# One core's hybrid attention and HGRN2 layer: products of 512 columns over both token streams, and x and the context loaded first

## The chip, the cores and the metric

The kernel runs on one core of one Trainium2 chip. The metric is the device time of one execution in microseconds (us); the time before is the median of three runs.

## The reference

One layer over 256 latent tokens `x` with a prefix of 256 context tokens `ctx`, all in float32, model width 2048. Both token streams are normed, modulated and multiplied by the same input weights. Only the latent stream goes on to attention queries, gates, output projection and SwiGLU.

```python
mod = silu(c) @ w_mod + b_mod                 # 2048 x 12288
mod_c = silu(c_ctx) @ w_mod + b_mod
h  = modulate(rmsnorm(x, g0), sh_a, sc_a)
hc = modulate(rmsnorm(ctx, g0), csh_a, csc_a)
p, pc = h @ w_in, hc @ w_in                   # q, kv and rope latents, HGRN2 q, ff, fb, i, g, two gates
attn_l = block_attention(q_l, [k_c, k_l], [v_c, v_l])
hgo_c, s_f, s_b = hgrn2_bidirectional(ctx parts, 0, 0)
hgo_l = hgrn2_bidirectional(latent parts, s_f, s_b)
out = (sig(gate0) * (attn_l @ w_br_mla) + sig(gate1) * (norm(hgo_l) * silu(g) @ w_br_hgrn)) @ w_out
x = x + gt_a * rmsnorm(out, g1)
h = modulate(rmsnorm(x, g2), sh_f, sc_f)
x = x + gt_f * rmsnorm((silu(h @ w_a) * (h @ w_b)) @ w_ffn_out, g3)
```

## The kernel before

Everything is float32. An operand of a large product is split into a rounded part H (ScalarE's cast to fp32r) and a rest L (VectorE's subtraction), and a product is the sum of three: H with H, H with L, L with H. Tokens lie on the free axis: a stream's h for one of the 16 blocks k of 128 model rows is a tile of 128 partitions by 2 parts by 256 tokens. The latent stream's 16 tiles are `hA`, the context's 16 are `hB`.

**Start.** The first modulation (`w_mod`'s columns for shift and scale of the first norm) comes in 32 tiles of 1 MB (`raw<-in_wm_dram`), in the groups of `GROUPS`: a group of nk blocks has 2·nk tiles. TensorE multiplies each tile with c (`pm`, L256). At the end of a group ScalarE copies the sum (`row`, L266), TensorE turns it (`pt`, L269), and VectorE and ScalarE make h of the group's blocks for both streams (L195 to L197). Meanwhile six blocks of 128 output columns of `w_in` (`pre`, whose weights come in 16 pieces `rw<-in_wst_dram` on GpSimd's queue) are built up block k by block k in six PSUM banks (L125, called from `pre_mm`). The norms of x and ctx (`norm_x`) are squares on ScalarE, sums on VectorE, a product with ones (`ptok`, L143), and a product that spreads the root over the partitions (`pbc`, L155).

**Heads.** Then come the attention latents and the eight HGRN2 heads. Each head has five blocks of `w_in` of 128 columns (`project`); three of them are for both streams, two for the latent stream alone. Of the blocks for both streams, those of the latents of k and v, of the rope part and of head 0 are `pre`; heads 1 to 7 have 21 more. For each k a block for both streams has six products of 256 columns (`mm3`, L125), a block for one stream three. VectorE's chains of the forget gate run beside it.

**Gates, attention, merge, output, SwiGLU.** The 32 gate blocks (`gates`) use `mm_wide` (one product of 512 columns over H and L side by side, L129, and one of 256, L130). Their results wait in 16 tiles `sgt` until the merge (L713 to L719). Output projection and the second half of the SwiGLU (`project_tok`, L778) have products of 512 columns.

The order on each engine comes from a scheduler that simulates the program at build time; the queues run in that order. Raw weights (`raw`) have three buffers of 1 MB, filled by SyncE's queue.

## Time and profile before

| | |
|---|---|
| median of 3 runs | 1767.45 us (1766.27 to 1767.64) |
| the profiled execution | 1768.12 us, of which its span 1766.30 us |
| TensorE (PE) busy | 1725.0 us, 98% of the span |
| weight loads (PEld) busy | 1528.4 us, 87% |
| VectorE (DVE) busy | 1110.0 us, 63% |
| ScalarE (ACT) busy | 800.1 us, 45% |
| moved by DMA | 374.64 MB, mean 212 GB/s |

A busy PE says only that products lie one behind the other: each row's duration has its draining in it, which the next product overlaps. What a product costs is read from the distance of two starts. Between the end of the span's last instruction and the device time lie 1.82 us that no view shows.

### The profile page before, as it was taken

How to read it: one execution, taken by the hardware profiler on the slowest of the kernel's cores; microseconds unless marked ns; L12 is line 12 of the kernel's file. 1: busy time of each engine (PE TensorE's matmuls, PEld its weight loads, DVE VectorE, ACT ScalarE, POOL GpSimd, SP SyncE). 2: the span in 40 equal slices, each digit the busy share in tenths (PEclk: the TensorE clock that was granted, in tenths of full speed). 3: DMA queues.
4: the chain of work that ended last, by engine and by line, in shares of the span. 5: the costliest groups of instructions: out<-in, count | busy, mean ns of one | idle time of the engine just before them, and what ended most of it. 6: DMA issues, size and time to landing. Idle time of an engine off the chain costs nothing.

```text
span 1766.3 us, 26819 instructions
## 1 busy us (share of the span) xinstructions
PE 1725.0 (98%) x10976; PEld 1528.4 (87%) x10976; DVE 1110.0 (63%) x1703; ACT 800.1 (45%) x1178; POOL 38.6 (2%) x57
## 2 busy tenths in 40 slices
PE   4999999999999999999999899999999999999998
PEld 2779999999999888888998698888888888888886
DVE  4335777766678766666775687776445555555556
ACT  4224433333334655555444554444444444334443
POOL 2100000000000000000110000000000000000000
PEclk9999999999999999999999999999999999999999
DMA  9985456555556555566765457777555555555563
GB/s 361 331 320 194 140 178 208 191 191 170 175 173 231 212 182 207 177 248 232 260 228 200 169 178 275 281 276 257 195 192 185 188 191 190 192 191 189 181 215 130
DMA packets 56459, 374.64 MB, mean 212 GB/s; under 512 B 6512, under 2 KB 6800, under 8 KB 13072
## 3 DMA queue, kind: packets, MB, share of 16 engines
q1 hardware_dynamic: 53424, 365.06, 59.1%
q0 software_dynamic: 2048, 6.29, 1.1%
q8 instruction: 86, 1.41, 0.3%
q10 hardware_dynamic: 864, 1.57, 0.2%
q14 instruction: 37, 0.30, 0.0%
HBM read 370.79 MB, written 2.11 MB: 211 GB/s over the span
## 4 chain that ended last, share of the span: by engine, by line
PE 97%; DVE 1%; DMA 1%; ACT 1%; issue 0%; SPq 0%; DVEq 0%; ACTq 0%
PE ps L125 20%; PE pst L778 18%; PE psf L129 18%; PE psf L130 9%; PE ps L129 7%; PE psb L713 5%; PE pre L125 4%; PE ps L130 3%; PE pm L256 2%; PE psf L872 1%; PE psS L656 1%; PE po L679 1%; PE psS L653 1%; DMA xt<-in_xT_dram 1%; PE pv L628 1%; PE pq L612 1%
## 5 line engine op out<-in xcount | busy, mean ns | idle before, releaser
L102 DVE TENSOR_TENSOR wL<-raw,wH 128x1024 fp32r<-128x1024 f32 (+1 forms) x492 | 597.5, 1217 | 462.4 <-ACT wH L100 461.3
L100 ACT CAST wH<-raw 128x1024 fp32r<-128x1024 f32 (+1 forms) x492 | 508.7, 1037 | 748.7 <-PE ps L125 182.1
L129 PE MATMUL psf<-h,wH 128*128 128x512 f32 x1344 | 475.1, 399 | 0.0
L130 PE MATMUL psf<-h,wL 128*128 128x256 f32 x1344 | 377.5, 281 | 0.0
L129 PEld LDWEIGHTS psf<-h,wH 128*128 128x128 f32 x1344 | 252.6, 188 | 62.8
L125 PE MATMUL ps<-hA,wH 128*128 128x256 f32 x1312 | 254.6, 285 | 0.0
L130 PEld LDWEIGHTS psf<-h,wL 128*128 128x128 f32 x1344 | 253.9, 189 | 0.2
L125 PEld LDWEIGHTS ps<-hA,wH 128*128 128x128 f32 x1312 | 204.8, 192 | 1.2 <-issue 0.5
L125 PE MATMUL ps<-hA,wL 128*128 128x256 f32 x656 | 187.3, 286 | 0.0
L129 PE MATMUL ps<-hA,wH 128*128 128x512 f32 x512 | 183.8, 400 | 0.0
L778 PE MATMUL pst<-wH,gA 128*128 128x512 f32 x576 | 166.6, 389 | 0.0
L321 DVE CUSTOM_DVE_ANT_0 raw<-raw,cb 128x2048 f32<-128x2048 f32 x64 | 146.0, 2281 | 29.9 <-DMA raw<-in_wm_dram 29.7
L130 PE MATMUL ps<-hA,wL 128*128 128x256 f32 x512 | 144.0, 282 | 0.0
L125 PE MATMUL ps<-hB,wH 128*128 128x256 f32 x672 | 137.2, 284 | 0.0
L778 PEld LDWEIGHTS pst<-wH,gA 128*128 128x128 f32 x576 | 108.0, 188 | 22.3
L125 PEld LDWEIGHTS ps<-hA,wL 128*128 128x128 f32 x656 | 125.7, 192 | 0.5 <-issue 0.5
L129 PEld LDWEIGHTS ps<-hA,wH 128*128 128x128 f32 x512 | 96.0, 188 | 22.9 <-issue 1.3
L125 PEld LDWEIGHTS ps<-hB,wH 128*128 128x128 f32 x672 | 105.0, 192 | 0.0
L778 PE MATMUL pst<-wL,gA 128*128 128x512 f32 x288 | 101.4, 389 | 0.0
L130 PEld LDWEIGHTS ps<-hA,wL 128*128 128x128 f32 x512 | 96.5, 189 | 2.6 <-DVE mx L658 1.1
L125 PE MATMUL ps<-hB,wL 128*128 128x256 f32 x336 | 95.2, 283 | 0.0
L778 PE MATMUL pst<-wH,mg 128*128 128x512 f32 x256 | 74.4, 389 | 0.0
(432 smaller groups left out, 2189.3 us busy)
## 6 DMA issues: line engine op xcount, KB each, us to landing
raw<-in_wm_dram SPq DMA_DIRECT2D x96, 1024.0 KB, 5.0
raw<-in_wfi_dram SPq DMA_DIRECT2D x84, 1024.0 KB, 4.9
raw<-in_win_dram SPq DMA_DIRECT2D x73, 1024.0 KB, 4.9
raw<-in_wfo_dram SPq DMA_DIRECT2D x44, 1024.0 KB, 4.8
raw<-in_wbr_dram SPq DMA_DIRECT2D x16, 1024.0 KB, 5.0
raw<-in_wout_dram SPq DMA_DIRECT2D x16, 1024.0 KB, 4.9
rw<-in_wst_dram POOLq DMA_DIRECT2D x16, 256.0 KB, 5.8
raw<-in_wqk_dram SPq DMA_DIRECT2D x4, 1024.0 KB, 4.9
```

Of the source, the lines that this page charges most:

```text
L100: nc.scalar.copy(H, raw[:, o:o + n])
L102: nc.vector.tensor_tensor(L, raw[:, o:o + n], H.bitcast(F32), op=ALU.subtract)
L125: nc.tensor.matmul(o, l, r, start=(first and i == 0), stop=(last and i == len(seq) - 1))
L129: nc.tensor.matmul(ps, w[0], act.rearrange("p e t -> p (e t)"), start=first, stop=False)
L130: nc.tensor.matmul(ps[:, 0:T], w[1], act[:, 0, :], start=False, stop=last)
L256: nc.tensor.matmul(pm[32 * (k % 4):32 * (k % 4) + 32, 0:n], cst[:, k], raw[:, kk * n:(kk + 1) * n], start=(k < 4), stop=(k >= KD - 4))
L321: nc.vector.tensor_tensor_reduce(out=raw, in0=raw, in1=cbt[0], scale=1.0, scalar=0.0, op0=ALU.mult, op1=ALU.add, accum_out=mod2[:, i // KD ...
L612: nc.tensor.matmul(pq[:, i * T:(i + 1) * T], l, r, start=(k == 0 and i == 0 and z == 0), stop=(k == 3 and i == 1 and z == 2))
L628: nc.tensor.matmul(pv[:, i, :], ckvs[:, k, l, ts_], r, start=(i == 0 and k == 0 and z == 0), stop=(i == 1 and k == 1 and z == 2))
L653: nc.tensor.matmul(psS, qn[a][:, i * T + qb * P:i * T + (qb + 1) * P], kn[b], start=(n == 0), stop=False)
L713: nc.tensor.matmul(ps[:, br * T:(br + 1) * T], l, r, start=(br == 0 and k == 0 and z == 0), stop=(br == 1 and k == NH - 1 and z == 2))
L778: mm = nc.tensor.matmul(ps[hf], l, r, start=(k == 0 and n == 0), stop=(k == nk - 1 and n == 2))
```

## The change

Both streams' h go into one tile `hx` of 128 partitions by stream, block k, part and 256 tokens. A block for both streams now has, for each k, three products of 512 columns; their moving operand is two runs of 256 columns, one of each stream, which lie 32 KB apart on a partition. SyncE's queue loads x and the context before the first tiles of the modulation, and the weights of blocks k = 0 and 1 too; `GROUPS` begins with four groups of one block instead of two. The norm is spread by one product with ones whose result stands in every partition; root and reciprocal are then taken over 128 x 256. As the h tiles are gone, other tiles move: the gate blocks' results go to HBM (`sgd`) from a ring of four and come back at the merge, and merged products, second h, the SwiGLU's products and some weights use parts of `hx`. The diff, cut to its core:

```diff
-GROUPS = [1, 1, 2, 2, 2, 2, 2, 2, 2]
+GROUPS = [1, 1, 1, 1, 2, 2, 2, 2, 2, 2]
...
+    hx = cp.tile([P, 2, KD, 2, T], F32R, name="hx")
+    def both(k, e):
+        return hx[:, :, k, e, :]
...
-        rs.append(rstd_tok([acc[:, 0:T], acc[:, T:2 * T]], D, ("rstd", "ot")[s]))
+        ss = px.tile([P, 512], F32, tag="px", name="ssx")
+        for i in range(2):
+            nc.tensor.matmul(ss[:, 0:T], ones, acc[:, i * T:(i + 1) * T], start=(i == 0), stop=(i == 1))
+        rs.append(rstd_from(ss[:, 0:T], D, T, ("rstd", "ot")[s]))
...
     def pre_mm(ws, k, b):
-        mm3([pre[b][:, 0:T], pre[b][:, T:2 * T]], ws(b * P, P),
-            [(hs[s][k][:, 0, :], hs[s][k][:, 1, :]) for s in range(2)], k == 0, k == KD - 1)
-    ahead = [load_w(wm1[0])]
-    load_x(xT)
-    ahead.append(load_w(wm1[1]))
-    load_x(ctxT)
+        mm3([pre[b].rearrange("p (s t) -> p s t", s=2)], ws(b * P, P), [(both(k, 0), both(k, 1))],
+            k == 0, k == KD - 1)
+    load_x(xT)
+    load_x(ctxT)
+    ahead = [load_w(wm1[0]), load_w(wm1[1])]
+    load_first(0, nc.sync)
+    ahead.append(load_w(wm1[2]))
+    load_first(1, nc.sync)
+    norm_x(0)
...
-        made += range(k0, k0 + nk)
         k0 += nk
-        if g == 0:
-            continue
-        if g == 1:
-            norm_x(1)
-        for k in made:
-            held += start_operands(k)
-        made = []
+        for k in range(k0 - nk, k0):
+            (todo if g < 2 else held).extend(start_operands(k))
...
-        outs = [ps[:, s * T:(s + 1) * T] for s in streams]
         for k in range(KD):
-            mm3(outs, w(k * P, P), [(hs[s][k][:, 0, :], hs[s][k][:, 1, :]) for s in streams], k == 0, k == KD - 1)
+            if len(streams) == 2:
+                o, act = ps.rearrange("p (s t) -> p s t", s=2), (both(k, 0), both(k, 1))
+            else:
+                o, act = ps[:, 0:T], (hx[:, 0, k, 0, :], hx[:, 0, k, 1, :])
+            mm3([o], w(k * P, P), [act], k == 0, k == KD - 1)
...
+    sgx = bp.tile([P, 8, 512], F32, tag="b16", name="sgx")
+    sgd = dp.tile([KD, P, 512], F32, name="sgd")
...
+        if b % 2 == 1:
+            nc.gpsimd.dma_start(sgd[j], sgx[:, j % 4, :])
...
     for j in range(KD):
+        sg = sgx[:, (4 + j) % 8, :]
+        nc.gpsimd.dma_start(sg, sgd[j])
```

How the instructions move on TensorE is shown at three places. In the rows, `ps` and `pre` are the sums of a block, `wH` and `wL` the parts of its weights, `hA`, `hB` and `hx` the streams' h. First, two steps of k in a block for both streams of the heads, before:

```order
L125 MATMUL ps<-hA,wH 128x256 x2
L125 MATMUL ps<-hB,wH 128x256 x2
L125 MATMUL ps<-hA,wL 128x256
L125 MATMUL ps<-hB,wL 128x256
L125 MATMUL ps<-hA,wH 128x256 x2
L125 MATMUL ps<-hB,wH 128x256 x2
L125 MATMUL ps<-hA,wL 128x256
L125 MATMUL ps<-hB,wL 128x256
```

Two steps of k in the same place now:

```order
L136 MATMUL ps<-hx,wH 128x512 x2
L136 MATMUL ps<-hx,wL 128x512
L136 MATMUL ps<-hx,wH 128x512 x2
L136 MATMUL ps<-hx,wL 128x512
```

Six products of 256 columns have become three of 512. Second, the first rows of TensorE's program, before (`pm` is a tile of the modulation, `pt` the turned sum, `ptok` and `pbc` the norm):

```order
L256 MATMUL pm<-raw,cst 32x256 x8
L143 MATMUL ptok<-ones,acc 128x1 x4
L256 MATMUL pm<-raw,cst 32x256 x8
L155 MATMUL pbc<-dg,ones 128x128 x2
L269 MATMUL pt<-c_84,row 128x2 x2
L125 MATMUL pre_95<-hA,wH 128x256
L125 MATMUL pre_96<-hA,wH 128x256
```

The first rows now (`ssx` is the norm of one stream):

```order
L212 MATMUL ssx<-acc,ones 128x256 x2
L290 MATMUL pm<-raw,cst 32x256 x8
L212 MATMUL ssx<-acc,ones 128x256 x2
L290 MATMUL pm<-raw,cst 32x256 x8
L303 MATMUL pt<-c_84,row 128x2 x2
L290 MATMUL pm<-raw,cst 32x256 x8
L136 MATMUL pre_96<-hx,wH 128x512
L136 MATMUL pre_97<-hx,wH 128x512
```

Both norms now stand ahead of the first product with h, and a third tile of the modulation too. Third, the end of a group of two blocks in the middle of the start (k = 6, 7), before:

```order
L125 MATMUL pre_100<-hA,wH 128x256 x2
L125 MATMUL pre_100<-hB,wH 128x256 x2
L125 MATMUL pre_100<-hA,wL 128x256
L125 MATMUL pre_100<-hB,wL 128x256
L269 MATMUL pt<-c_84,row 128x2 x4
L256 MATMUL pm<-raw,cst 32x512 x8
L125 MATMUL pre_95<-hA,wH 128x256
```

The same end now, and the end of the group of k = 3 ahead of it, whose rows are the last four:

```order
L136 MATMUL pre_101<-hx,wL 128x512
L290 MATMUL pm<-raw,cst 32x512 x4
L303 MATMUL pt<-c_84,row 128x2 x4
L290 MATMUL pm<-raw,cst 32x512 x8
L136 MATMUL pre_96<-hx,wH 128x512
...
L290 MATMUL pm<-raw,cst 32x256 x8
L303 MATMUL pt<-c_84,row 128x2 x2
L290 MATMUL pm<-raw,cst 32x512 x4
L136 MATMUL pre_96<-hx,wH 128x512
```

Before, products with h stood between a group's last tile and `pt`; now `pt` stands straight behind the tile, and in the groups of one block one tile instead of two stands between `pt` and the first product that needs the new h.

## Rows read from the trace of the kernel before

**Rows 1.** The page: busy time of each engine, and the chain of work that ended last by engine.
```profile
PE 1725.0 (98%) x10976; PEld 1528.4 (87%) x10976; DVE 1110.0 (63%) x1703; ACT 800.1 (45%) x1178; POOL 38.6 (2%) x57
...
PE 97%; DVE 1%; DMA 1%; ACT 1%; issue 0%; SPq 0%; DVEq 0%; ACTq 0%
```

**Rows 2.** Stretches of the span: from and to, length, busy time of PE, PEld, DVE, ACT and POOL (number of instructions), granted clock of TensorE, share of the DMA engines, GB/s.
```profile
0.00:43.50 43.50, 20.16 (x121) 10.93 (x121) 20.44 (x54) 20.71 (x41) 9.43 (x21) 0.93 0.94 360
43.50:68.30 24.80, 24.04 (x194) 18.19 (x194) 7.08 (x19) 6.12 (x14) 3.19 (x6) 0.98 0.88 323
68.30:141.50 73.20, 72.21 (x575) 53.81 (x574) 28.35 (x73) 20.55 (x42) 5.34 (x10) 1.00 0.91 335
...
230.00:549.00 319.00, 319.00 (x2674) 318.64 (x2673) 228.02 (x463) 113.19 (x150) 0.00 (x0) 1.00 0.55 186
```

**Rows 3.** TensorE in order of time, in a block for both streams of a head: start, duration, line, operands, count.
```profile
318.78 0.28 PE L125 MATMUL ps<-hA,wL 128*128 128x256 f32 x1
318.90 0.28 PE L125 MATMUL ps<-hB,wL 128*128 128x256 f32 x1
319.02 0.40 PE L125 MATMUL ps<-hA,wH 128*128 128x256 f32 x2
319.26 0.40 PE L125 MATMUL ps<-hB,wH 128*128 128x256 f32 x2
319.49 0.28 PE L125 MATMUL ps<-hA,wL 128*128 128x256 f32 x1
```

**Rows 4.** The same view where products of 512 columns follow each other: the keys of attention, and the output projection.
```profile
597.47 0.61 PE L125 MATMUL pk<-cqkv,wH 128*128 128x512 f32 x2
597.92 0.39 PE L125 MATMUL pk<-cqkv,wL 128*128 128x512 f32 x1
598.15 0.61 PE L125 MATMUL pk<-cqkv,wH 128*128 128x512 f32 x2
...
959.92 0.39 PE L778 MATMUL pst<-wL,mg 128*128 128x512 f32 x1
960.15 0.61 PE L778 MATMUL pst<-wH,mg 128*128 128x512 f32 x2
960.61 0.39 PE L778 MATMUL pst<-wL,mg 128*128 128x512 f32 x1
```

**Rows 5.** The same view where products of 512 and of 256 columns take turns.
```profile
1403.09 0.40 PE L129 MATMUL psf<-h,wH 128*128 128x512 f32 x1
1403.34 0.28 PE L130 MATMUL psf<-h,wL 128*128 128x256 f32 x1
1403.45 0.40 PE L129 MATMUL psf<-h,wH 128*128 128x512 f32 x1
```

**Rows 6.** TensorE in order of time at the start; in brackets the idle time before and what ended it.
```profile
8.27 1.93 PE L256 MATMUL pm<-raw,cst 128*32 128x256 f32 x16 [8.27 <-DMA raw<-in_wm_dram]
19.54 1.87 PE L143 MATMUL ptok<-ones,acc 128*128 128x1 f32 x8 [9.34 <-DVE acc L188]
28.07 1.22 PE L125 MATMUL pre<-hA,wH 128*128 128x256 f32 x4 [3.00 <-ACT hA L196]
39.01 1.94 PE L256 MATMUL pm<-raw,cst 128*32 128x512 f32 x8
43.47 1.18 PE L125 MATMUL pre<-hB,wH 128*128 128x256 f32 x4
44.59 1.06 PE L256 MATMUL pm<-raw,cst 128*32 128x512 f32 x8
```

**Rows 7.** What the DMA engines moved in the first 60 us, in 40 slices of 1.5 us.
```profile
GB/s 0 197 289 388 400 403 341 415 410 415 442 415 410 418 429 421 431 437 423 434 426 366 281 188 355 388 423 254 251 415 388 437 382 257 60 246 431 350 328 216
```

**Rows 8.** VectorE's reciprocal over 128 x 256, and the load of one piece of `wst` (from the page: KB, median us from issue to landing).
```profile
L135 DVE RECIPROCAL rstd<-rstd 128x256 f32<-128x256 f32 x4 | 7.0, 1743 | 0.0
...
rw<-in_wst_dram POOLq DMA_DIRECT2D x16, 256.0 KB, 5.8
```

**Rows 9.** TensorE in order of time where the start's groups end: `pt`, what follows it, and the first product that needs the new h.
```profile
50.09 1.07 PE L256 MATMUL pm<-raw,cst 128*32 128x512 f32 x8
51.91 1.05 PE L269 MATMUL pt<-c,row 128*128 128x2 f32 x8 [0.76 <-ACT row L266]
67.37 0.95 PE L269 MATMUL pt<-c,row 128*128 128x2 f32 x8
68.25 1.07 PE L256 MATMUL pm<-raw,cst 128*32 128x512 f32 x8
...
84.06 1.92 PE L256 MATMUL pm<-raw,cst 128*32 128x512 f32 x16
86.15 1.43 PE L125 MATMUL pre<-hA,wH 128*128 128x256 f32 x7 [0.16 <-ACT hA L196]
...
140.54 0.95 PE L269 MATMUL pt<-c,row 128*128 128x2 f32 x8
143.00 1.62 PE L125 MATMUL pre<-hA,wH 128*128 128x256 f32 x7 [1.51 <-ACT hA L196]
144.85 0.41 PE L125 MATMUL pre<-hB,wH 128*128 128x256 f32 x1
145.06 0.41 PE L125 MATMUL pre<-hA,wH 128*128 128x256 f32 x1
```

**Rows 10.** Stretches as in rows 2, cut where the granted clock changes.
```profile
37.60:44.50 6.90, 6.18 (x24) 2.34 (x24) 2.50 (x8) 1.28 (x3) 0.54 (x1) 0.51 0.89 337
44.50:143.40 98.90, 95.66 (x760) 71.50 (x760) 36.71 (x97) 27.58 (x58) 8.53 (x16) 1.00 0.90 333
143.40:146.90 3.50, 3.50 (x18) 3.44 (x18) 1.77 (x5) 0.74 (x2) 1.67 (x2) 0.51 0.73 309
```

More of the change, by code (lines that the diff above doesn't have):

```diff
@@ L110, in split_w, with split_into, get @@
         return get
+    def split_into(raw, tiles):
+        for i, (H, L) in enumerate(tiles):
+            nc.scalar.copy(H, raw[:, i * 512:(i + 1) * 512])
+            nc.vector.tensor_tensor(L, raw[:, i * 512:(i + 1) * 512], H.bitcast(F32), op=ALU.subtract)
+        def get(o, n):
+            return tuple(t[:, o % 512:o % 512 + n] for t in tiles[o // 512])
+        return get
     def split_act(dst, src, heng=None):
@@ L188, in norm_x @@
                 nc.vector.tensor_tensor(acc, acc, sq, op=ALU.add)
-        rs.append(rstd_tok([acc[:, 0:T], acc[:, T:2 * T]], D, ("rstd", "ot")[s]))
+        ss = px.tile([P, 512], F32, tag="px", name="ssx")
+        for i in range(2):
+            nc.tensor.matmul(ss[:, 0:T], ones, acc[:, i * T:(i + 1) * T], start=(i == 0), stop=(i == 1))
+        rs.append(rstd_from(ss[:, 0:T], D, T, ("rstd", "ot")[s]))
     def make_h(k):
-        for s, tag in ((0, "hA"), (1, "hB")):
-            h = ap.tile([P, 2, T], F32R, tag=tag, name=tag)
+        for s in range(2):
+            h = hx[:, s, k]
             xk = xs[s][:, k, :]
@@ L705, in block_kernel @@
     mg = []
+    units = [hx[:, 1, 8 + j] for j in range(8)] + [hx[:, 0, j] for j in range(8)]
+    spare = [hx[:, 1, j] for j in range(8)] + [hx[:, 0, 8 + j] for j in range(8)]
     for j in range(KD):
+        sg = sgx[:, (4 + j) % 8, :]
+        nc.gpsimd.dma_start(sg, sgd[j])
         w = split_w(load_w(wbr[j]))
@@ L744, in gate_rows @@
         nc.sync.dma_start(gdr[i], grow)
-        tiles = []
-        for c in range(4):
-            g = ap.tile([P, 512], F32, tag=tag, name="gbc", bufs=bufs)
+        for c, g in enumerate(tiles):
             nc.sync.dma_start(g, gdr[i, 4 * c:4 * c + 4].rearrange("k p -> (k p)").partition_broadcast(P))
-            tiles.append(g)
         return tiles
@@ L792, in rstd_part, with pairs @@
         return rt
-    g1b = gate_rows(0, "hC", 8)
+    def pairs(tiles):
+        return list(zip(tiles[0::2], tiles[1::2]))
+    g1b = gate_rows(0, [ap.tile([P, 512], F32, tag="hC", name="gbc", bufs=8) for _ in range(4)])
     x1 = bp.tile([P, 2, D], F32, tag="b16", name="x1")
@@ L802, in block_kernel @@
         cs = slice(c * 512, (c + 1) * 512)
-        ps = project_tok(lambda q: wout[c, q], KD, mg, True, True, ("hB", 16) if c == 3 else None)
+        ps = project_tok(lambda q: wout[c, q], KD, mg, True, True,
+                         pairs([wide(u) for u in spare[:8]]) if c == 3 else None)
         for hf in range(2):
@@ L811, in block_kernel @@
             sqrt_table(ssq[:, 0, 0, 0:1])
-    wfs0 = split_w(load_w(wfs[0]), step=512, tags=("hB", "hB"), pool=ap, bufs=16)
+    wfs0 = split_into(load_w(wfs[0]), pairs([wide(u) for u in spare[8:]]))
     xsc = [[None] * 4, [None] * 4]
@@ L897, in swish @@
         else:
-            g = ap.tile([P, 2, T], F32R, tag="hA", name="gA")
+            g = spare[n_g[0] % 16]
+            n_g[0] += 1
         split_act(g, sa)
@@ L910, in ffn_out @@
             ps = project_tok(lambda q: wfo[c, q0 + q], 4 * nq, G[4 * q0:], part == 0, part == 2,
-                             ("hC", 8) if part == 2 and c == 3 else None)
+                             pairs([ap.tile([P, 512], F32R, tag="hC", name="wl", bufs=8) for _ in range(8)])
+                             if part == 2 and c == 3 else None)
             for hf in range(2):
@@ L937, in block_kernel @@
         if part == 2:
-            g2b = gate_rows(1, "hB", 16)
+            g2t = cp.tile([P, 4, 512], F32, tag="cst", name="g2t")
+            g2b = gate_rows(1, [g2t[:, c] for c in range(4)])
         ffn_out(part)
```

51 lines of the change are left out of this document (29 added, 22 removed).

## The prediction

> **What bounds the kernel now.** First the page. TensorE is busy for 98% of the span, and the chain of work that ended last runs through it for 97% [rows 1]. Then the stretches, for a busy TensorE need not be at its peak. In the heads (230 to 549 us) it is busy throughout at the full clock, VectorE for 71% of the time, the DMA engines for 55% [rows 2]; so this stage lasts as long as its products need, and nothing else has to be faster. From 43.5 us to the end of the start TensorE is busy too, at a DMA share of 0.88 to 0.91, and before 43.5 us it is idle for more than half of the time [rows 2]. What a product costs is the distance of two starts. In a block for both streams the starts lie 0.12 us apart (318.78, 318.90, 319.02, then two products to 319.26) [rows 3]; I take 120 ns.
>
> **Part 1: 512 columns in the heads.** A step of k in a block for both streams is six products of 256 columns, 6 x 120 = 720 ns. The trace has the new form, three products of 512 columns with the same operand order, in the keys of attention: 597.47 to 597.92 is two, 597.92 to 598.15 one, and in the output projection 960.15 to 960.61 is two [rows 4]. That is 225 to 230 ns; I take 228, so a step costs 684 ns, 36 less. Heads 1 to 7 have 21 such blocks of 16 steps, 336 in all: 336 x 36 ns = 12.1 us. Bounds: at 226 ns the gain is 14.1 us. Where products of 512 and 256 take turns, the one of 512 takes 0.24 to 0.25 us (1403.09 to 1403.34; the one of 256 behind it 0.11, to 1403.45) [rows 5]; at 240 ns the gain is nothing. I take the value of the like form. Blocks for one stream and everything behind the heads keep their products. Nothing in the trace has a moving operand of two pieces; that is a rival below.
>
> The gap between products is where a rule and the rows part. By the Trainium skill (TensorE: Matmul & The Clock Gate, Back-to-back issue gap) an isolated product takes its columns over 2.4 GHz plus a fixed 2.5 ns at full clock. By that a step would go from 6 x 109.2 to 3 x 215.8 ns and save 7.8 ns, an estimate of 2.6 us in the heads. The trace does not agree: it has some 11 ns more for each product, of 256 columns or of 512, and three products fewer in a step save that three times; the rows decide.
>
> **Part 2: the start.** It has 96 more steps of this kind. First, when can it begin? x and the context are 4.2 MB, and constants and one piece of weights that travel beside them 1.0 MB. Some 0.3 MB move in the first 3 us and 0.4 MB per us after that [rows 7], so both streams are there at 3 + (5.2 - 0.3)/0.4 = 15 us, the first tile (1.05 MB) at 18, the second at 21, the third at 24. Before, the first tile came at 8.27 and the latent stream's norm at 19.54 [rows 6]. The context's norm is now multiplied behind tile 1 (1.9 us at the low clock [rows 6]), at 20 us. Then come a root on ScalarE that stands behind the casts of the first weights (landing at about 22), the reciprocal over 256 columns, 1.74 us where it was one over two numbers [rows 8], and h: I put the first product with h at 28 us. That is where it was (28.07), but now for both streams; before, the context's products began at 43.47 [rows 6].
>
> From there I add up to the `pt` of k = 4, 5, which ended at 68.25 [rows 9]. Block 0, with tile 4 of the modulation and much of it at the low clock, to 35.5. A `pt` is 0.5 us, h is ready some 2.1 us behind a `pt` (84.06 to 86.15 [rows 9]), 18 products are 4.1 us, a tile is 1.0. In the groups of one block `pt` stands straight behind the tile, with 0.8 to 0.9 us of waiting for ScalarE's copy (51.91, idle 0.76 [rows 9]), and one tile covers 1.0 of the 2.1 us. So k = 1 ends at 35.5 + 0.5 + 2.1 + 4.1 = 42.2; k = 2 with the next tile at 42.2 + 0.5 + 2.1 + 4.1 + 1.0 + 0.9 = 50.8; k = 3 with three tiles at 50.8 + 0.5 + 2.1 + 4.1 + 3.0 + 0.9 = 61.4; `pt` to 62.4. That is 5.9 us ahead.
>
> Then five groups of two blocks; they took 73.2 us. Each now has 36 x 228 = 8.2 us of products for 72 x 120 = 8.6: 2.2 us less, and 0.4 in the last blocks. Against this, in the group of k = 4, 5 one tile stands behind `pt` instead of two (1.0 us), and `pt` behind the last tile costs about 0.8 in one more group: 2 us. And idling costs clock: behind the 1.51 us of waiting at 143.00 the granted clock fell to 1.2 GHz until 146.9 [rows 10], and a product of 256 took 0.21 us instead of 0.12 (144.85 to 145.06 [rows 9]), 16 x 0.09 = 1.5 us. The new waits behind `pt` are alike; I count two such stretches, 3 us. Part 2: -5.9 - 2.2 - 0.4 + 2 + 3 = -3.5 us. Bounds: without any of the waits -8.5; with the low clock up to the first group of two blocks, three more blocks of 18 products at twice 0.21 us instead of 0.23 (10.4 us) and eight tiles at 1.94 instead of 1.06 (7 us) [rows 6], less some 3 us of the waits inside, +11.
>
> **What costs nothing.** The gate blocks' results go to HBM and back: 32 transfers of 256 KB, of which one lands in 5.8 us [rows 8]; they have GpSimd's nearly idle queue, are read up to eight blocks ahead, and a block of the merge is 48 products, 5.8 us. Uncovered, one would cost up to 5.8 us. The first two gate blocks wait for head 7's scores, as their ring takes over the scans' tile; three other PSUM banks cover that, and without them it is about 1 us. The load order moves `wst` past nothing but the norms on SyncE's queue. The tiles that move to `hx` have the same operations.
>
> **Sum.** 1768.1 (the profiled execution, 0.7 above the median) - 12.1 - 3.5 = 1752.5, against the median 1752. I say **1752.5 us**.
>
> **The rivals.** *The start stays at the low clock.* For: before 44.5 us the low clock was granted in 37.6 to 44.5, after an idle stretch [rows 10], and the new groups of one block idle more often. Against: on 44.5 to 143.4 it held in spite of waits of 0.2 to 0.8 us [rows 9, 10]. Part 2 is then +11, and the time 1768.1 - 12.1 + 11 = 1767; with part of it, about 1760. *Products of 512 are no cheaper than two of 256.* At 240 ns the 336 and the 96 steps lose their 36 ns each, 12.1 and 3.5 us: 1768. For: rows 5. Against: rows 4, the same form. The issue gap of the Trainium skill named above would be near to this, with an estimate of 1762.6. *The two-piece operand makes each product slower.* This is the rival on the other side: the place is the 1008 products of the heads and 288 of the start. Each ns over 228 costs 1.3 us, so from 240 ns all is lost, and at 250, ten more for the jump from one stream's run to the other's, it is 1752.5 + 28.5 = 1781. For: no row has such an operand. Against: a run is 256 columns long and PSUM is written in one run, as before. By the Trainium skill (Advanced Engine Details and Errata, SBUF Cachelines) what costs is an access that leaves the 16 bytes of the one before it; a single jump in 512 columns would not show. No row here tests that. *The start gains all it could.* h is ready in time, the clock holds: part 2 is -8.5 or better, 1747 and below.
>
> **Chances.** The forecast (1747 to 1758) 0.65; the start at the low clock in part or whole (1758 to 1768) 0.14; no cheaper products 0.06; slower products 0.07; the better start 0.08. The measurement of this kernel can tell about 0.2% (3.5 us) from no change, that is 1764 to 1771. Faster: 0.65 + 0.08 + 0.10 + 0.02 = 0.85; the same: 0.04 + 0.04 = 0.08; slower 0.07. The range that leaves out two in ten at most: 1745 to 1764 us.
>
> **What would show it.** Starts of the products over both streams 0.225 to 0.23 us apart in the heads; a head some 1.7 us shorter (three blocks of 16 steps); both norms done by 26 us and the first product over both streams near 28; the last `pt` near 134 to 138 us instead of 140.5; waits of 1 to 2 us behind each `pt` of one block, and short stretches at 1.2 GHz behind some of them; no waits in the merge. The prediction is wrong if these starts lie 0.24 us or more apart, if the clock stays low up to 60 us, or if a transfer of the gate blocks shows as what TensorE waits for.

## The result, and the profile after

The changed kernel takes 1769.97 us (median of 20 executions, 1766.96 to 1773.91), the kernel before 1766.89 (20 executions, 1765.14 to 1769.66). The ratio is 1.0018, with an interval of 1.0012 to 1.0024: 0.2% slower, where 1752.5 was forecast and the range ended at 1764. The profiled execution of the changed kernel took 1770.05 us, its span 1768.3.

The page of the changed kernel: busy time of each engine, and the chain by engine, as in [rows 1].

```profile
PE 1719.5 (97%) x9696; PEld 1455.7 (82%) x9696; DVE 1114.2 (63%) x1702; ACT 781.7 (44%) x1162; POOL 55.6 (3%) x85
...
PE 96%; DMA 2%; DVE 1%; ACT 1%; issue 0%; DVEq 0%; SPq 0%; ACTq 0%
```

TensorE is still the bound, and it has 1280 products fewer. So the first question is what one product costs now. From start to start, in rows of TensorE in order of time (start, duration, line, operands, count), a block for both streams of a head:

```profile
317.62 0.62 PE L136 MATMUL ps<-hx,wH 128*128 128x512 f32 x2
318.08 0.40 PE L136 MATMUL ps<-hx,wL 128*128 128x512 f32 x1
318.32 0.63 PE L136 MATMUL ps<-hx,wH 128*128 128x512 f32 x2
```

Two products take 0.46 us and one 0.24. Over 859 of them in the heads the mean is 233.2 ns, where the forecast had 228. That alone is 5 us lost. The larger loss stands where the forecast had no term at all. In the second half of the SwiGLU the stationary operand is a tile g, which lies either in an `hC` tile (as it did before) or in a part of `hx`; line and moving operands are the same for both. Four stretches of some 48 products each, `hC`, `hx`, `hC`, `hx` in turn (from and to, length, busy time and number of products and of weight loads, granted clock, DMA share, GB/s; a product on an edge is counted on both sides):

```profile
1489.51:1500.42 10.92, 10.91 (x48) 9.02 (x49) 1.00 0.52 194
1500.42:1511.66 11.24, 11.24 (x49) 9.04 (x48) 1.00 0.54 187
1511.66:1522.56 10.89, 10.89 (x49) 9.01 (x48) 1.00 0.54 194
1522.56:1533.80 11.24, 11.24 (x49) 9.04 (x48) 1.00 0.55 187
```

With `hC` 48 products take 10.9 us, 227 ns each; with `hx` they take 11.24, 234 each, at the same clock and DMA share. So the place of an operand costs 7 ns a product. The other way round, a step of 512 and 256 columns got cheaper, 0.35 us from 1439.11 to 1439.46, while before they came to 0.36 in [rows 5] and to 353.3 ns in the mean of the SwiGLU:

```profile
1439.11 0.39 PE L140 MATMUL psf<-hx,wH 128*128 128x512 f32 x1
1439.34 0.28 PE L141 MATMUL psf<-hx,wL 128*128 128x256 f32 x1
1439.46 0.39 PE L140 MATMUL psf<-hx,wH 128*128 128x512 f32 x1
```

Where the 2.0 us of the span come from, by the distances of starts added up in each stage of the two profiled executions (after minus before): from the start to the first product of the latents (`ps`) −1.2; latents, heads, gates and attention −2.7; merge −0.1; output projection and second half of the SwiGLU (`pst`) +9.2; first half of the SwiGLU (`psf`) −5.3; end of the program +2.1. In the second of these, products over both streams gave 336 x (719.2 − 699.7) = 6.5 us, two new waits took 3 us back, and 0.8 is spread over the rest. The waits:

```profile
167.33 0.39 PE L136 MATMUL ps<-hx,wL 128*128 128x256 f32 x1 [1.21 <-DVE wL L102]
174.44 0.50 PE L136 MATMUL ps<-hx,wH 128*128 128x256 f32 x2 [1.33 <-ACT lat L380]
```

Behind them is ScalarE's order, here in the changed kernel:

```profile
157.40 1.28 ACT L336 ACT_TABLE_LOAD   x1
158.69 1.92 ACT L336 ACTIVATE cbs<-cb 128x2048 f32<-128x2048 f32 x1
160.63 1.28 ACT L145 ACT_TABLE_LOAD   x1
161.92 0.69 ACT L145 ACTIVATE ktn<-ss,epst 128x512 f32<-128x512 f32 x1
```

The scheduler now puts the sigmoid of c (`cbs`) and two table loads ahead of the root `ktn`, which in the kernel before ran at 158.74. VectorE's reciprocal and the splits behind it come 3 us later.

At the end of the program, the last operations stand where they stood (GpSimd's last sum starts at 1760.78, before at 1760.88), but the span ends 2 us later. The last line of the kernel on GpSimd's queue (times of one in ns, shortest, median, longest), before and after:

```profile
L1071 POOLq DRAIN  x3: 45/102/4472, 1760.8 to 1766.0; - x3
```

```profile
L1117 POOLq DRAIN  x3: 45/93/6757, 1760.7 to 1768.0; - x3
```

GpSimd's drain lasts 6.76 us instead of 4.47, and all engines wait for it. Its queue has had 60 transfers instead of 32: the 32 of `sgd` were added, four weights of blocks 0 and 1 went to SyncE.

The start was 5 us ahead in the middle, as forecast, and then lost it (TensorE in order of time):

```profile
29.39 2.37 PE L136 MATMUL pre<-hx,wH 128*128 128x512 f32 x6 [0.35 <-ACT hx L220]
...
62.47 1.05 PE L303 MATMUL pt<-c,row 128*128 128x2 f32 x8 [0.76 <-ACT row L300]
65.51 1.93 PE L290 MATMUL pm<-raw,cst 128*32 128x512 f32 x8 [1.99 <-DMA raw<-in_wm_dram]
...
97.43 1.07 PE L290 MATMUL pm<-raw,cst 128*32 128x512 f32 x8 [0.76 <-DMA raw<-in_wm_dram]
100.58 1.07 PE L290 MATMUL pm<-raw,cst 128*32 128x512 f32 x8 [0.49 <-DMA raw<-in_wm_dram]
...
127.23 1.07 PE L290 MATMUL pm<-raw,cst 128*32 128x512 f32 x8 [0.66 <-DMA raw<-in_wm_dram]
```

TensorE now waits for the tiles of the modulation. In the view of its waits from 28 to 150 us (in all, times, longest) that is a row, which the kernel before does not have at all:

```profile
PE pm L290 <- DMA raw<-in_wm_dram: 4.5, 5, 2.0
```

The stretches around these waits, with the granted clock and the DMA share in the last columns but one:

```profile
65.10:68.50 3.40, 2.99 (x11) 1.16 (x12) 2.11 (x6) 1.08 (x3) 0.00 (x0) 0.50 1.01 429
68.50:140.10 71.60, 67.64 (x371) 40.36 (x369) 25.35 (x65) 18.73 (x38) 4.25 (x8) 1.00 0.84 317
140.20:147.00 6.80, 6.22 (x15) 4.86 (x16) 2.36 (x6) 1.33 (x4) 1.90 (x2) 0.50 0.77 323
```

TensorE idles for 1.99 us up to 65.51; from 65.1 us on the granted clock is the low level of 1.2 GHz for 3.4 us, with the DMA engines full. Behind the last `pt` it is low for 6.8 us, before it was 3.4 [rows 10].

### The profile page after: what moved, and what is told of

Read it like the earlier page. It is cut to its first block, busy times and chain, and to the rows that moved or that the text cites. A ratio compares the mean times of both kernels' runs of the same rounds, so it can differ in the third digit from the quotient of the medians.

```text
span 1768.3 us, 24307 instructions
## 1 busy us (share of the span) xinstructions
PE 1719.5 (97%) x9696; PEld 1455.7 (82%) x9696; DVE 1114.2 (63%) x1702; ACT 781.7 (44%) x1162; POOL 55.6 (3%) x85
## 4 chain that ended last, share of the span: by engine, by line
PE 96%; DMA 2%; DVE 1%; ACT 1%; issue 0%; DVEq 0%; SPq 0%; ACTq 0%
PE ps L136 20%; PE pst L816 19%; PE psf L140 18%; PE psf L141 9%; PE ps L140 7%; PE psb L754 5%; PE pre L136 4%; PE ps L141 3%; PE psf L915 1%; PE pm L290 1%; DMA raw<-in_wm_dram 1%; PE psS L692 1%; PE po L716 1%; PE psS L689 1%; PE pv L664 1%; PE pq L648 1%
## 5 line engine op out<-in xcount | busy, mean ns | idle before, releaser
L102 DVE TENSOR_TENSOR wL<-raw,wH 128x1024 fp32r<-128x1024 f32 x480 | 588.2, 1227 | 458.4 <-ACT wH L100 456.6
L100 ACT CAST wH<-raw 128x1024 fp32r<-128x1024 f32 x480 | 501.6, 1046 | 745.2 <-PE ps L136 194.7
L140 PE MATMUL psf<-hx,wH 128*128 128x512 f32 x1344 | 470.8, 393 | 0.0
L141 PE MATMUL psf<-hx,wL 128*128 128x256 f32 x1344 | 374.9, 279 | 0.0
L136 PE MATMUL ps<-hx,wH 128*128 128x512 f32 (+1 forms) x1312 | 334.1, 343 | 1.3 <-ACT lat L380 1.3
L140 PEld LDWEIGHTS psf<-hx,wH 128*128 128x128 f32 x1344 | 251.8, 187 | 60.0
L141 PEld LDWEIGHTS psf<-hx,wL 128*128 128x128 f32 x1344 | 251.8, 187 | 0.3
L136 PEld LDWEIGHTS ps<-hx,wH 128*128 128x128 f32 x1312 | 225.0, 188 | 31.3 <-ACT lat L380 1.5
L816 PE MATMUL pst<-wH,hx 128*128 128x512 f32 x800 | 237.2, 396 | 0.0
L136 PE MATMUL ps<-hx,wL 128*128 128x512 f32 (+1 forms) x656 | 225.1, 343 | 1.2 <-DVE wL L102 1.2
L140 PEld LDWEIGHTS ps<-hx,wH 128*128 128x128 f32 x512 | 96.0, 188 | 23.2 <-issue 1.7
L136 PEld LDWEIGHTS pre<-hx,wH 128*128 128x128 f32 x192 | 37.5, 201 | 26.0 <-ACT hx L220 10.9
```

What stands on the lines that cost most here:

```text
L100: nc.scalar.copy(H, raw[:, o:o + n])
L102: nc.vector.tensor_tensor(L, raw[:, o:o + n], H.bitcast(F32), op=ALU.subtract)
L136: nc.tensor.matmul(o, l, r, start=(first and i == 0), stop=(last and i == len(seq) - 1))
L140: nc.tensor.matmul(ps, w[0], act.rearrange("p e t -> p (e t)"), start=first, stop=False)
L141: nc.tensor.matmul(ps[:, 0:T], w[1], act[:, 0, :], start=False, stop=last)
L816: mm = nc.tensor.matmul(ps[hf], l, r, start=(k == 0 and n == 0), stop=(k == nk - 1 and n == 2))
```

## The experiments

Times are medians; ratios are to the kernel before, on the same chip.

**Is it where hx starts?** In the programs' allocation `hA`, `hB`, `hC`, `wH` and `wL` of the kernel before all start at one residue of 256 bytes on a partition. `hx` starts 96 bytes behind that residue. Two kernels move tiles by 32 bytes, with not one instruction or its order changed. In the first, the tile ahead of `hx` moves it by 32 bytes, and both small tiles together move all that is allocated behind them, the weights too, by 64; so `hx` comes from 96 to 64 bytes behind the weights' residue.

```diff
+    pad0 = cp.tile([P, 8], F32, name="pad0")
     hx = cp.tile([P, 2, KD, 2, T], F32R, name="hx")
+    pad1 = cp.tile([P, 8], F32, name="pad1")
```

> The changed kernel with hx moved by 32 bytes on each partition (a tile of 32 bytes ahead of it, another behind it), so that it starts at a multiple of 64 bytes as hA, hB and hC did before; every instruction and its order are the same. In the changed kernel the products of 512 of output projection and SwiGLU start 230 to 238 ns apart where the stationary operand is a part of hx, and 226 to 227 ns where it is an hC tile, in the same stage and with the same moving operands. Theory (the start address): with hx they come to 226 to 227 ns too, about 1250 products x 7.6 ns = 9.5 us; the products over both streams, 232 ns, come to about 228, 1296 x 4 = 5 us; the step of the gate blocks and of the first half of the SwiGLU (512 and 256 columns), which went from 353 to 350 ns with the change, goes back to 353 if that is the address too, 1856 x 3.3 = 6 us. Net 8 to 15 us faster than the changed kernel, at about 1755 to 1762. Rival (it is not the address: one large tile, or its place beside other tiles, or the transfers of that stage): all distances stay and the time is that of the changed kernel, 1770.

Measured: 1764.64 us, ratio 0.9987 (0.9978 to 0.9996), 5.3 us below the changed kernel. Products over both streams take 229.2 ns, those with a part of `hx` stationary 233.3 instead of 234.2, the SwiGLU's steps of 512 and 256 352.3 instead of 350.0. So it is the place, since nothing else was changed; but a multiple of 64 bytes is not the rule, for the products with h stationary hardly moved.

For the kernel before, the pool of `hA`, `hB` and `hC` gets the same pads (a pool with 8 columns ahead of it, one behind it):

```diff
+    ap0 = ctx.enter_context(tc.tile_pool(name="ap0", bufs=1))
     ap = ctx.enter_context(tc.tile_pool(name="ap", bufs=16))
+    ap1 = ctx.enter_context(tc.tile_pool(name="ap1", bufs=1))
```

> The kernel before with the pool of hA, hB and hC moved by 32 bytes, so that these tiles start 32 bytes behind a multiple of 64; every instruction and its order are the same. Theory (the start address): the products of 512 of output projection and SwiGLU go from 227 to about 234 ns, 1440 x 7.6 = 11 us; the steps of gate blocks and first half of the SwiGLU go from 353 to 350 ns, 6 us less if that is the address too; the products of 256 about as before. Net 5 us slower than the kernel before, 11 if the steps stay. Rival (not the address): nothing changes, 1767.

Measured: 1752.54 us, ratio 0.9924 (0.9911 to 0.9936), 14 us faster. The sign of the expectation was wrong. The products with h stationary did become slower, 233 ns, but those of 256 columns went to about 117 ns and the steps of 512 and 256 to 347. So each form has a best place of its own, and the kernel before did not have it either.

**A map.** What counts then may be the distance between the starts of the two operands. One kernel measures it with nothing beside it; `hb` and `wx` are two tiles at rest, and each form is run at 44 pairs of offsets.

```diff
+    def two(wo, ho):
+        ws, wm, h = rows(wo, ho)
+        ps = bank("two")
+        o = ps.rearrange("p (s t) -> p s t", s=2)
+        run([(o, ws(k, a), h[:, :, k, b]) for k in range(KD) for a, b in ((0, 0), (0, 1), (1, 0))])
...
+    for wo, ho in OFFS:
+        one(wo, ho)
+        two(wo, ho)
+        wide(wo, ho)
+        tok(wo, ho)
```

> A kernel that computes nothing of the layer: it repeats the four forms of product of this kernel, some 48 at a time from operands that lie still in SBUF, with no transfers beside them, and moves the start of h by d bytes against the start of the weights (both on one residue of 1024 bytes at d = 0, as hA, hB, hC and the weights were in the kernel before). Forms: one (256 columns of h, weights stationary), two (two runs of 256 columns, as the blocks over both streams now), wide (512 and 256 in turns, as the gate blocks), tok (512 columns of weights, h stationary, as output projection). Forty-four places: d from 0 to 992 in steps of 32, then the weights moved by 32 and 64 as well, then d of 4, 8, 16 and 48. Theory (the distance between the two operands' starts decides, whatever else runs): one is 120 ns at d = 0 and 117 at d = 32; tok is 227 at d = 0, 232 at 32, 231 at 64, 234 at 96; two is 229 at 64 and 232 at 96; wide is 353 a step at d = 0, 346 at 32 and 350 at 64 and 96; with both moved by 32 or 64 the values follow the distance. Second theory (the start of h alone decides): with the weights moved the values follow h's own residue. Rival (what else reads and writes SBUF decides): all places give the same number for one form, within 1 ns.

The rows of the first two places, distances 0 and 32 (TensorE in order of time, one row for a form at one place; `wide` counts its products of 512 columns first):

```profile
64.86 5.92 PE L76 MATMUL one<-hb,wx 128*128 128x256 f32 x48
70.61 11.07 PE L76 MATMUL two<-hb,wx 128*128 128x512 f32 x48
81.52 5.80 PE L76 MATMUL wide<-hb,wx 128*128 128x512 f32 x32
87.16 11.07 PE L76 MATMUL tok<-wx,hb 128*128 128x512 f32 x48
98.07 5.76 PE L76 MATMUL one<-hb,wx 128*128 128x256 f32 x48
103.67 11.36 PE L76 MATMUL two<-hb,wx 128*128 128x512 f32 x48
114.87 5.72 PE L76 MATMUL wide<-hb,wx 128*128 128x512 f32 x32
120.43 11.36 PE L76 MATMUL tok<-wx,hb 128*128 128x512 f32 x48
131.62 3.58 PE L76 MATMUL one<-hb,wx 128*128 128x256 f32 x29
```

From start to start, 48 products of `one` take 5.75 us (119.8 ns each) at distance 0 and 5.60 (116.7) at 32; of `two` 10.91 (227.3) and 11.20 (233.3). The same from all rows, in ns (first to last start of a form; `wide` for a step of two products):

| distance h − w, bytes | one | two | wide | tok |
|---|---|---|---|---|
| 0 | 119.8 | 227.3 | 352.7 | 227.2 |
| 32 | 116.7 | 233.3 | 347.3 | 233.3 |
| 64 | 117.9 | 229.0 | 348.9 | 233.5 |
| 96 | 119.8 | 233.3 | 350.7 | 234.1 |
| 128 | 119.9 | 233.3 | 350.7 | 232.2 |
| 160 | 118.7 | 234.2 | 347.9 | 233.6 |
| 192 | 113.6 | 233.2 | 353.1 | 228.9 |
| 224 | 118.3 | 233.2 | 353.1 | 233.2 |
| 4 | 123.2 | 240.0 | 360.1 | 232.5 |
| 16 | 118.7 | 231.6 | 347.7 | 226.7 |

From 256 to 992 bytes the table repeats itself to 0.2 ns. With both operands moved by 32 or 64 the values of the same distance come back, to 0.7 ns, with one exception (`one` at a distance of 192 with the weights moved by 64: 117.9). So, but for that exception, the distance decides, modulo 256 bytes, and no other engine, transfer or clock is needed for it (the granted clock of this run is 1.00). The kernel before has distance 0, the best for `two` and `tok` and nearly the worst for `one` and `wide`; the changed kernel has 96, the worst for `tok` and a bad one for `two`. Why the chip does so, no run here shows.

**The change without its displacement.** `h0` sets `hx` 160 bytes further, to distance 0.

```diff
+    pad0 = cp.tile([P, 40], F32, name="pad0")
     hx = cp.tile([P, 2, KD, 2, T], F32R, name="hx")
+    pad1 = cp.tile([P, 24], F32, name="pad1")
```

> The changed kernel with hx 160 bytes further (96 bytes of padding behind it), so that hx and the weights wH, wL lie on the same residue of 256 bytes, as hA, hB and the weights did in the kernel before; instructions and order are the same. By the distances of the run map (theory: they hold inside the kernel too) against the changed kernel, whose distance was 96: products over both streams 233.3 to 227.3 ns, 1296 x 6 = 7.8 us less (1.7 of it in the start, where it may not count); the products of 512 with h stationary 234.1 to 227.2, 1248 x 6.9 = 8.6 us less; the steps of 512 and 256 from 350.7 to 352.7, 1856 x 2 = 3.7 us more. Net 11 to 12.7 us: 1757 to 1759. Rival (other readers and writers of SBUF blur it): half of it or less, 1763 or more.

Measured: 1758.34 us, ratio 0.9952 (0.9939 to 0.9966): 11.6 us below the changed kernel, as the map had it. In its heads:

```profile
317.75 0.61 PE L136 MATMUL ps<-hx,wH 128*128 128x512 f32 x2
318.21 0.39 PE L136 MATMUL ps<-hx,wL 128*128 128x512 f32 x1
318.44 0.61 PE L136 MATMUL ps<-hx,wH 128*128 128x512 f32 x2
318.89 0.39 PE L136 MATMUL ps<-hx,wL 128*128 128x512 f32 x1
```

A step is 0.68 us; the mean of 841 products is 227.8 ns. That is 336 x (719.2 − 683.4) = 12.0 us of gain against the kernel before, the forecast's 12.1. The forms `two` and `tok` follow the map to 1 ns in the kernels. Steps of 512 and 256 do not always: the gate blocks take 349.6 ns at distance 0 (map 352.7), the SwiGLU 352.3 at distance 64 (`al64`; map 348.9).

**The end and the two waits.** `sgd` on ScalarE's queue:

```diff
-            nc.gpsimd.dma_start(sgd[j], sgx[:, j % 4, :])
+            nc.scalar.dma_start(sgd[j], sgx[:, j % 4, :])
...
-        nc.gpsimd.dma_start(sg, sgd[j])
+        nc.scalar.dma_start(sg, sgd[j])
```

> The changed kernel with the gate results' 32 transfers on ScalarE's queue instead of GpSimd's. At the end of the program GpSimd drains; its drain ended 5.0 us behind its last operation in the changed kernel (60 transfers on its queue) and 2.7 us in the kernel before (28), and the span's end came 2.0 us later though the last operations stand at the same time. Theory (the drain grows with the transfers that this queue had): the drain falls to 2.7 us or less, the span ends with the output's landing, 2 us earlier, at about 1768. Rival (the drain is chance of one execution, or of the program's end): it stays near 5 us and the time at 1770.

The drain of this run:

```profile
L1117 POOLq DRAIN  x3: 45/93/4146, 1765.7 to 1771.1; - x3
```

The drain is 4.15 us, and from GpSimd's last operation to the end of the span it is 3.87 us instead of 5.77: the theory holds. (The expectation gave 28 transfers for the kernel before; it has 32, and 28 are those of this run.) With 28, 32 and 60 transfers the drain is 4.15, 4.47 and 6.76 us, 0.08 us for each transfer; the 13 profiles of the layer (four with 28, four with 32, five with 60) have these three values to 5 ns. The time, 1769.52 us (ratio 1.0019, 1.0010 to 1.0027), shows only 0.5 of the 2 us. In its profile the start ended 3 us later, and the merge, from its first product to that of the output projection, took 94.2 us instead of 92.1, with waits for weights. The other kernels with these transfers on ScalarE's queue have a longer merge too: `h0_fix` 94.3 and `g_old` 93.3 against `h0` 92.2, `best_a` 91.7 against `best` 89.2. So moving the transfers may have cost there what the drain gave back; that is not shown, for `cb_late`, which did not move them, has 93.6.

`cb_late` binds `make_cb` behind the reciprocal of the latents' norm:

```diff
-    make_cb()
+    with tc.issue_after(kvrec.ins):
+        make_cb()
```

> The changed kernel with the sigmoid of c and its product (cbs, cb) bound to come behind the reciprocal of the k and v latents' norm, as the order of the kernel before had it. In the changed kernel they come ahead, with two table loads on ScalarE, and TensorE waits 1.48 us at 167.33 and 1.61 us at 174.44 for weights and latents. Theory (the order costs these waits): both are gone, 3.1 us less, about 1767. Rival (the waits are the start's arrears, which would show a little later): other waits of like size within 30 us, no change.

Measured: 1772.82 us, ratio 1.0036 (1.0023 to 1.0050), worse. The bond holds on VectorE alone, so ScalarE still had the sigmoid first, and VectorE had to wait for the late root with nothing to do: a gap of 3.5 us from start to start in place of 1.5 and 1.6. It does not speak for or against the order as the cause, since the order on ScalarE was not changed. `h0_fix` binds both engines, and takes `h0` and `sgd_act` in:

```diff
+    with tc.issue_after(kv_root.ins), tc.issue_after(kv_rec.ins):
+        make_cb()
```

> h0 with two things undone besides: the gate results' transfers go through ScalarE's queue (run sgd_act), and the sigmoid of c is bound behind the root of the k and v latents' norm on ScalarE and its product behind the reciprocal on VectorE (in run cb_late only VectorE's product was bound, and ScalarE still had the sigmoid and two table loads ahead of the root). Expected: GpSimd's drain gives back 2 us at the end, the waits of 1.48 and 1.61 us near 167 and 174 go, 5 us less than h0, about 1753; this would be the forecast of 1752.5 with the start's term at nothing. Rival for the waits: as in cb_late, one of like size comes in their place, then 1756.

Measured: 1756.54 us, ratio 0.9940 (0.9928 to 0.9953). Between 150 and 180 us no gap of 0.7 us or more is left, the stage from the latents to the merge is 2.4 us shorter than in h0, and the drain is short, but only 1.8 of the expected 5 us show in the median; the ranges overlap (1753.81 to 1758.14, h0 1754.99 to 1762.75). The time is the rival's, though no wait came in the place of the two. In the profile its start ends 1.5 us later than h0's (`pw` at 152.06 and 150.55), and the merge takes 2.0 us more, 1.1 of them in three waits for weights.

**What bounds the start?** `half` is h0 with half of each modulation tile loaded; it leaves out the other half, so its result is not the layer's.

```diff
+    def load_h(src):
+        raw = wp.tile([P, 2048], F32, tag="raw", name="raw")
+        nc.sync.dma_start(raw[:, 0:1024], src[:, 0:1024])
...
-                    nc.tensor.matmul(pm[32 * (k % 4):32 * (k % 4) + 32, 0:n], cst[:, k], raw[:, kk * n:(kk + 1) * n],
+                    nc.tensor.matmul(pm[32 * (k % 4):32 * (k % 4) + 32, 0:n], cst[:, k], raw[:, kk * n % 1024:kk * n % 1024 + n],
```

> h0 with only the first 1024 of the 2048 columns of each tile of the first modulation loaded, and the products that need the others multiplying these again (the modulation is then not the reference's): 16 MB less to load in the start, the same number of products on TensorE. In h0 TensorE waits for tiles (raw<-in_wm_dram) at 60, 64.5, 82, 96.8, 99.8 and 125.8 us, 4 to 6 us in all, behind the early start, and the start ends no earlier than before. Theory (the transfers bound the start, so the gain of the early products is given back): these waits go, and the rope's product pw, which marks the start's end (150.6 in h0, 151 to 158 in the other profiles of the changed kernel), comes at 145 or earlier; the time is 5 to 10 us below h0, about 1750. Rival (the chain tile, copy, pt, h and the products with h bounds it): pw stays within 2 us of h0's.

Measured: 1746.96 us, ratio 0.9889 (0.9874 to 0.9904), and the start's end, `pw`, moves to

```profile
141.77 0.59 PE L402 MATMUL pw<-kr,cn 128*128 128x256 f32 x2
```

that is 8.8 us ahead of h0. Of the waits for tiles one is left, 1.65 us at 80.67. Its first product with h comes later than h0's (31.14 and 28.64), so the gain is made behind it; the stretch at 1.2 GHz that followed a wait for a tile in h0 (65.9 to 69.3 us) is gone as well. The transfers bind the start of the changed kernel: what TensorE gains there, it waits for the next tile. The waits at 163 and 170 of h0 are gone in this kernel too, which makes up 3 of the 11.4 us; here the scheduler put the root ahead of the sigmoid:

```profile
145.89 0.69 ACT L150 ACTIVATE ktn<-ss,epst 128x512 f32<-128x512 f32 x1 [1.49 <-PE ss L390]
146.59 1.28 ACT L343 ACT_TABLE_LOAD   x1
147.89 1.92 ACT L343 ACTIVATE cbs<-cb 128x2048 f32<-128x2048 f32 x1
```

With `h0_fix` that makes two kernels with this order and without the waits.

`g_old` is h0_fix with the old groups:

```diff
-GROUPS = [1, 1, 1, 1, 2, 2, 2, 2, 2, 2]
+GROUPS = [1, 1, 2, 2, 2, 2, 2, 2, 2]
```

> h0_fix with GROUPS as in the kernel before (two groups of one block, then groups of two), with the new order of loads and the products of 512 kept. Theory (the transfers bound the start): the waits for tiles get fewer, as the products with h come in larger portions, and the start ends where it does in h0_fix, within 1.5 us (pw at 152.1 there); the time is 1755 to 1758. Rival 1 (the groups of one block are what costs the 3.5 us, by their waits behind pt and the clock that falls behind them): 3 us or more faster, 1753. Rival 2 (they are what keeps the start from being longer): 4 us or more slower.

Measured: 1754.72 us, ratio 0.9931 (0.9919 to 0.9944), `pw` at 151.78. The start ends within 0.3 us of h0_fix in the profile, and the times overlap. The time lies 0.3 us below the theory's range, and the waits for tiles did not get fewer (six, 5.0 us, where `h0_fix` has four, 3.4 us); they stand elsewhere. The groups of one block neither win nor lose a measurable time.

**Is a product of 512 worth anything?** `b192` is the kernel before with the pads of `b32` at 192 and 64 bytes.

> The kernel before with hA, hB and hC 192 bytes further (64 bytes of padding behind), instructions and order the same. By the run map at a distance of 192: products of 256 columns 119.8 to 113.6 ns, about 3300 with weights and h so placed, 20.5 us less (2 of it in the start), half of the merge's 768 and the SwiGLU's first 192 products another 3.6; the products of 512 with h stationary 227.2 to 228.9, 2.4 us more; the steps of 512 and 256 0.4 more, 0.7 us. Net 19 to 21 us: 1746 to 1748. This says whether products of 512 over both streams are worth anything: six of 256 at 113.6 are 681.6 ns, three of 512 at 227.3 are 681.9. Rival (the map does not carry over): 1760 or more.

Measured: 1752.08 us, ratio 0.9917 (0.9903 to 0.9931). In its heads 256 columns take 114.2 ns (0.11 from start to start):

```profile
318.13 0.39 PE L127 MATMUL ps<-hA,wH 128*128 128x256 f32 x2
318.36 0.39 PE L127 MATMUL ps<-hB,wH 128*128 128x256 f32 x2
318.59 0.28 PE L127 MATMUL ps<-hA,wL 128*128 128x256 f32 x1
318.70 0.28 PE L127 MATMUL ps<-hB,wL 128*128 128x256 f32 x1
318.81 0.39 PE L127 MATMUL ps<-hA,wH 128*128 128x256 f32 x2
```

A step is 0.68 us (318.13 to 318.81), as with three products of 512 in h0. The total missed the expectation by 4 us. In the blocks of the latents ahead of the heads a product took 117.8 ns, the other value that the map has at this distance; the gate blocks' steps rose from 349.6 to 352.3 ns; the products with h stationary cost 3.1 us instead of 2.4; and the start gave 1.3.

`best` gives every product of the kernel before the best distance that its tiles allow: `h` as in `b192`, the weights' tiles 64 columns longer and begun further in by use (a small tile, `dg`, shares another's buffer to make room). `best_a` does the same to h0_fix.

```diff
-            H = pool.tile([P, n], F32R, tag=tags[0], name="wH", bufs=bufs)
+            q, m = (at[o // step], n + 64) if pool is wp else (0, n)
+            H = pool.tile([P, m], F32R, tag=tags[0], name="wH", bufs=bufs)[:, q:q + n]
...
-            w = split_w(load_w(wfi[2 * (j - 2) + i]))
+            w = split_w(load_w(wfi[2 * (j - 2) + i]), at=(40, 40))
...
-                ws.append(split_w(raw))
+                ws.append(split_w(raw, at=(48, 48)))
```

> The kernel before with each product at the best distance of the run map that its tiles allow: h 192 bytes further as in b192, and the weights' tiles 256 bytes longer, so that they start 160 bytes further for gate blocks and first half of the SwiGLU (distance 32: 352.7 to 347.3 ns a step, 1856 x 5.4 = 10 us less), 192 further for output projection and second half (distance 0: 227.2 ns as before), 64 further for the merge's attention half and the queries (distance 192). Instructions and order are the same as before. With the 20.5 of b192 for 256 columns, 4.8 for the merge, 1.8 for the rest: 35 to 37 us less than before, about 1730 to 1732. Rival: as in b192.

> h0_fix with the distances of the run best on the changed kernel's structure: weights' tiles 256 bytes longer, their start 64 bytes further for blocks of one stream, the merge, the queries and the SwiGLU's first blocks (distance 192), 224 further for gate blocks and first half of the SwiGLU (distance 32), unmoved for blocks over both streams and the products with h stationary (distance 0). Order as in h0_fix. By the run map: steps of 512 and 256 columns 5.4 ns less, 10 us; 960 products of one stream 1.9 to 6.2 ns less (the map shows both 113.6 and 117.9 at this distance), 1.8 to 6 us; merge 1.5 to 4.8; the rest 0.5 to 1.5. From 1756.5 to 1734 to 1743. Theory (with every product at its best distance three of 512 cost what six of 256 do, so the change of shape is worth nothing): within 0.3% of the run best, 1736.5. Rival (the new shape and start are worth something by themselves): 1731 or less.

Measured: `best` 1736.47 us, ratio 0.9831 (0.9818 to 0.9845), 30 us below the kernel before and the fastest of all that do the whole work. It missed 1730 to 1732 in the main because the blocks of the latents and the merge's half with `aT` took 117.8 ns a product instead of 113.6. The steps of 512 and 256 gave their 10 us, 8.9 of them in the SwiGLU's first half, where a step is 0.35 us (1300.23 to 1300.58):

```profile
1300.23 0.39 PE L132 MATMUL psf<-h,wH 128*128 128x512 f32 x1
1300.46 0.28 PE L133 MATMUL psf<-h,wL 128*128 128x256 f32 x1
1300.58 0.39 PE L132 MATMUL psf<-h,wH 128*128 128x512 f32 x1
```

`best_a` 1743.45 us, ratio 0.9868 (0.9855 to 0.9881): 0.4% above `best`, a little outside the 0.3% of the theory, and far from the rival's 1731. In its profile `pw` comes 6.2 us later than in `best` (158.41 and 152.23), and the merge waits four times for weights, 2.6 us in all. So the change as a whole wins nothing once the products have about their best distances; in these runs it is 0.4% behind. For the shape by itself the heads show it, where a step is 0.68 us either way. How much of the 0.4% is the start cannot be told, as it differs from kernel to kernel by as much.

## Why the prediction was wrong

**The step that failed** is the sentence "The tiles that move to `hx` have the same operations", under what costs nothing, and beside it "everything behind the heads keep their products". The operations were the same, their price was not: 234 instead of 227 ns with h stationary (+9.2 us), against which the steps of 512 and 256 gave 5.3 us in `psf`, more than nothing too. I took the cost of a product from its shape. The traces show that it hangs on where its operands start as well, by up to 6 ns in 120 and 13 in 227. Between the forecast (15.6 us less) and the profiled execution (2.0 more) lie 17.6 us: 9.4 from the latents to the attention (5.6 of them by the price of the products over both streams, 3 by the two waits), 9.2 with h stationary, 2.3 in the start and 2.1 at the program's end, less 5.3 in `psf` and 0.1 in the merge.

**Part 1, mechanism right, place not asked.** 228 ns was read from rows of the same shape [rows 4], and these rows have distance 0. At distance 0 the term is right to 0.1 us (h0). At 96 the products take 233.2 ns, and 12.1 us became 6.5. Rows 5, which bounded it at 240, lie at distance 0 as well: they are 512 and 256 columns in turns, a form of its own, of which the map has 352.7 ns a step there.

**The gap rule.** The Trainium skill's fixed 2.5 ns a product (TensorE: Matmul & The Clock Gate, Back-to-back issue gap) does not fit the traces: 256 columns take 113.6 to 123.2 ns at full clock, by the distance alone. The "some 11 ns more for each product" that I set against it is not a constant either; at distance 192 it is 4 ns with 256 columns. The time given for that rival, 1762.6, does not come out of the sum's own terms either: with 2.6 us in the heads it would be 1762.0, and with the start's 96 steps at the same 7.8 ns 1764.7.

**The two-piece operand** is free: `two` takes 227.3 ns at distance 0, `tok`, whose moving operand is one run, 227.2, and the keys' products, one run with the weights stationary as here, 0.68 us for three [rows 4]. The rival on the other side fell as to its mechanism, though its sign came true. The rival of a start at the low clock fell too: the granted clock was at the level of 2.4 GHz from 31 to 65 us.

**Part 2.** The first product with h came at 29.39 (forecast 28), and `pt` of k = 4, 5 began at 62.47 where the forecast had it end at 62.4: these steps held, the lead was 4.9 us of the forecast 5.9. The last `pt` began at 137.93, at the late end of "134 to 138". What the sum behind the lead had wrong is the bound: five groups were costed by TensorE's own work, although [rows 2] had the DMA share at 0.88 to 0.91 there. This stage had no room; 4.5 us went into waits for tiles, which the sum did not have, and the two clock stretches cost about what I had counted. From that `pt` to the first product of the latents 3.7 us were lost where the sum has 2.4 (2 and 3 less 2.2 and 0.4). Part 2 was −1.2 instead of −3.5 to the first product of the latents, and the rope behind it came 0.1 us earlier. It can't be told more exactly: over eight profiles with the new start (without `half`) that first product lies between 147.5 and 155.4 us, 151.6 in the mean, over four with the old one between 150.3 and 153.3, 151.9 in the mean.

**What costs nothing, again.** The transfers of `sgd` were hidden in the merge, as said; they cost 2 us at a place that I did not look at, the drain of the queue that issued them. The order of ScalarE around the latents was not in the prediction at all, although the program's order shows it ahead of any run; it cost 3 us, of which `h0_fix` gave 2.4 back.

With the products at distance 0 (h0) the change is 8 us faster than the kernel before, with drain and order mended as well (h0_fix) 10 us, 12 of which the heads give. That is the forecast's sign for the reason given, and 4 us above its time. In the mean of the profiles the start's 3.5 are missing, though in the profile of `h0_fix` the first product of the latents does come 4.2 us earlier than before, and its merge is 2.0 us longer.

## What to carry to other kernels

When a change moves a tile, compare the addresses of both operands before and after, modulo 256 bytes here, and take the price of a product from rows of the same shape at the same distance. Before reshaping a loop of products, try shifting one operand by 32 to 224 bytes: it changes no instruction, and here was worth 14 us of 1767 by itself and 30 with a distance for each use. In a stage whose DMA share is 0.9, ask whether work that TensorE saves will only be time that it waits, as it was here, and read a queue that takes extra transfers at the program's end too.

## What the runs showed that I had not expected

A product of 512 columns costs 226.7 to 240.0 ns and one of 256 113.6 to 123.2, at one clock and with nothing else running, by the distance of its operands' starts modulo 256 bytes; each form has another best distance. Six products of 256 columns at distance 192 (681.6 ns) cost what three of 512 at distance 0 do (681.9). GpSimd's last drain grew by 0.08 us for each transfer that its queue had issued in the whole program, though the last of the added ones had landed some 880 us before. What in the chip makes the distance count, and why one form has two values at distance 192, stays open.
